# A decoder layer on one core: order of the first transfers, of a product's partner, of a gate's three steps, of spills, and of two attention lanes

## The chip, the cores and the metric

The kernel runs on one core of a Trainium2 chip. The core has five engines that work side by side, each through its own list of instructions in order: TensorE (PE, matmuls; its weight loads are shown apart as PEld), VectorE (DVE), ScalarE (ACT), GpSimd (POOL) and SyncE (SP, which here only starts transfers). SP, ACT and POOL each start transfers (DMAs) on a queue of their own. Engines wait for one another through semaphores. The metric is the device time of one execution in microseconds (us).

## What is computed

One layer of a hybrid decoder trunk, in float32, for 256 tokens of width 2048: an RMS norm, one wide projection, a gated linear attention (GLA, branch a), a differential attention (branch b), two branch projections that two gates merge, an output projection, and a residual with a second norm.

```python
h = rmsnorm(x, pre_norm_g[l])
proj = h @ w_in[l]
(a_q, a_k, a_v, a_g, a_lr, b_q, b_k, b_v, b_g, m_a, m_b) = jnp.split(proj, offsets, axis=-1)
gk = jax.nn.log_sigmoid((a_lr @ gla_gk_w2[l] + gla_gk_b[l]).astype(jnp.float32)) / GATE_LOGIT_NORMALIZER
o_a = gla_chunked(a_q, a_k, a_v, gk)                 # 4 heads of 256 keys, 512 values
o_a = rmsnorm(o_a, gla_norm_g[l]).reshape(B, S, GLA_VAL_DIM) * jax.nn.silu(a_g)
y_a = o_a @ w_branch_a[l]
...
w = p[:, :, 0] - lam * p[:, :, 1]                    # p: two causal softmaxes of a head's scores
o_b = jnp.einsum('bhqk,bkhv->bqhv', w.astype(v.dtype), v)      # 16 heads of 128 values
o_b = rmsnorm(o_b, diff_norm_g[l]) * (1.0 - lam_init)
o_b = o_b.reshape(B, S, DIFF_VAL_DIM) * jax.nn.silu(b_g)
y_b = o_b @ w_branch_b[l]
merged = jax.nn.sigmoid(m_a) * y_a + jax.nn.sigmoid(m_b) * y_b
x = x + rmsnorm(merged @ w_out[l], post_norm_g[l])
```

## The kernel before

**Splits.** Every float32 matrix is cut into a high part (`hi`) and a rest (`lo`), and a product is made of three matmuls: hi by hi, hi by lo, lo by hi. Weights arrive by DMA in tiles called `raw` (or `a`, `b`, `c` in the sets); ACT makes `hi` (L261), DVE makes `lo` (L262), then PE uses both (L437, L449). One such step, a "half", is 1024 columns or fewer. `take` keeps three halves made ahead of PE, and `load` starts the transfers two ahead, on SP. The tokens are split once in the same way into eight tiles `xs` (`prep_x`, L299).

**Phases.** First `first_joint`: sixteen steps of K, each with its piece of weights and its 256 tokens by 128 rows of x, which are loaded as the steps come (`load_x`). While the first pieces arrive, PE runs eight matmuls on ones (L343). Then two groups of GLA values, during which the small operations wait in a list of tasks, a step of each of them after a step of PE: among them `forget_gate` (log-sigmoid of both halves `hf` of the gate's input `gp`: Abs, Exp, Ln on ACT, then one DVE operation a half, L562) and `sum_operands` (sums of x tiles for the sets, whose splits `s4`, `r1`, `s2`, `r3` are L615 on ACT and L616 on DVE).

**Sets.** The middle of the run is seven "sets" (0 to 6): blocks of 1024 output columns made with seven products of half size in place of eight (numbered 1, 3, 5, 6, 2, 7, 4 in their order; `block_products`). A product has two parts t and each part two halves, so a slot is (set, product, t). The weight sums that the products want are made by the DMA itself (`accumulate`, L198: POOL starts a transfer that adds to the tile `a` or `b`) and by DVE (L206). Products 1, 3, 5, 2 have PSUM banks of their own; 6, 7 and 4 go on in the bank of product 1, so that after product 6 DVE reads the bank (`gr`, first half), and after product 7 again (`gr`, second half, L773) before product 4 may write to it. `phase_steps` lays out the order: after the two halves of a slot comes one half of the other products (queries, keys and values of both branches, computed as channel by token, `half_channel`, 16 matmuls into a bank `bg`). I call that half the slot's partner. There are fewer partners than slots; the table `skip` names the slots that go without. PE keeps the order as written there (`pinned`). An engine's list is otherwise made by a scheduler which may move an instruction past others, except those that are marked to keep the program's order, among themselves.

**Spills.** Tiles wanted much later are written to DRAM and fetched back (`spill`, `fetch`, both on POOL's queue unless said). Before the last product of the last set, the four tiles q and k of the GLA scores are fetched (L134).

**Lanes.** Later, while PE runs the projections of the GLA gates, of the last heads and of branch a, two generators `diff_lane(0)` and `diff_lane(1)` compute the differential attention, two heads (`one`, `two`) of a pair at a time, each lane its own pairs. A lane's steps for PE, with my letters: S (`scores`, L996/L997, two banks `bg`), T (`turned`, L1021, transposes of the probabilities, one bank), W (`weighted`, L1032 to L1034, one bank), and O (`turned_out`, L1051, transposes of the finished pair `ogb`, one bank, read by ACT as `obh`, L501, and then DVE as `obl`, L502). They are pushed in between runs of 24 matmuls of the projections, one step of each lane in turn (`pump`). There are four banks with the tag `bg`, given out in turn; a step that wants the fifth waits until the first one has been read.

Of the kernel before, what the change touches and what calls it, by code (L numbers as in the profile page):

```python
# [29 lines left out]
SETS = 7  # L30
# [46 lines left out]
def phase_steps():  # L77

    keys = ["v4"] + [f"{name}{hf}{c}" for hf in range(2) for name in ("k", "q") for c in range(4)]
    keys += [f"{name}{g}{c}" for g in EARLY for pair in range(2) for name in ("dq", "dk") for c in (2 * pair, 2 * pair + 1)]  # L80
    other = [(key, r, h) for key in keys for r in range(4 if key == "v4" else 1) for h in range(2)]
    slots = [(s, prod, t) for s in range(SETS) for prod in PRODUCTS for t in range(2)]
    front = [(0, prod, t) for prod in PRODUCTS[:2] for t in range(2)]
    skip = [(SETS - 1, 7, 1), (SETS - 1, 4, 1)] + [(s, prod, 0) for prod in (4, 2) for s in range(SETS - 1, 0, -1)]
    skip = skip[: len(slots) + len(front) - len(other)]
    mixed = []
    for slot in slots:
        mixed += [("set", *slot, h) for h in range(2)]
        for _ in range((slot not in skip) + (slot in front)):
            mixed.append(other.pop(0))  # L90
    return mixed + other
# [3 lines left out]
def hybrid_kernel(ctx: ExitStack, tc, xt, xn, preg, postg, w, w2, gkb, glag, lamv, diffg, ident_d, causal_d, lmask_d, out):  # L95
# [30 lines left out]
    def spill(t, name):  # L126
        count[0] += 1
        d = dram.tile(list(t.shape), t.dtype, name=f"{name}_{count[0]}")
        pool.dma_start(d, t)
        return d  # L130

    def fetch(d, name, make, queue=pool):
# [77 lines left out]
    def load(j):  # L210
        key, r, h = seq[j]
        src, size = weights(key, r)
        n = size // 2
        early = key == "v0"
        if key == "v3" and r == 0:
            for i in range(2):
                link(0, "a", i)
        count[0] += 1
        raw = raws[key, r] = wpool.tile([P, 2048], F32, tag="raw", name=f"raw_{count[0]}")
        if j == 0:  # L220
            load_x(0, 1)
        cuts = (0, n // 2, n, size) if j == 0 else (0, n, size) if j == 2 else (0, size)
        for a, b in zip(cuts, cuts[1:]):
            i = sp.dma_start(raw[:, a:b], src[:, a:b])
            if early:
                tc.keep_in_program_order(i)
        if early:
            for kt in X_LOADS[j // 2]:
                load_x(kt, 4)
# [53 lines left out]
    def load_x(kt, n, queue=sp):  # L283
        tc.keep_in_program_order(queue.dma_start(xraw[kt // 4][:, kt % 4 : kt % 4 + n, :], xt[:, kt : kt + n, :]))

    act.dma_start(preg_s, preg)
    load_x(1, 1, act)
    load_x(2, 2, act)
    act.preload_act_table_set("natural_log_exp_and_others")

    def x_ops(kt):
# [226 lines left out]
    def forget_gate():  # L518
        w2_raw = w2_tile[0]
        yield  # L520
        bank = ps("bg")
        for b in range(2):
            pe.transpose(bank[:, P * b : P * b + P], lr[:, b, :], ident)
        top = t2([P, 512], "lrh").bitcast(F32R)
        lrt = sm([P, S], "lrt", F32R, bufs=1)
        act.activation(top[:, :S], bank[:, :S], AF.Copy)
        for i in (0, 64):
            act.activation(lrt[i : i + 32, :], bank[i : i + 32, :S], AF.Copy)
            r = slice(i + 32, i + 64)
            dve.tensor_tensor(out=lrt[r, :], in0=bank[r, :S], in1=f32(top[r, :S]), op=ALU.subtract)  # L530
        w2_s = lend("s2l", "w2_s", F32R)
        top = lend("r3h", "w2h", F32R)
        r = slice(64, P)
        late = tc.keep_in_program_order
        late(act.activation(w2_s[:64, :], w2_raw[:64, :], AF.Copy))
        late(act.activation(top[r, :], w2_raw[r, :], AF.Copy))
        late(dve.tensor_tensor(out=w2_s[r, :], in0=w2_raw[r, :], in1=f32(top[r, :]), op=ALU.subtract))
        yield
        gp.extend(u([P, 2, 4, P], "gp") for _ in range(2))
        for hf in range(2):  # L540
            for c in range(2):
                bank = ps("bg")
                for i in range(2):
                    ct = 4 * hf + 2 * c + i
                    o = bank[:, S * i : S * i + S]
                    pe.matmul(o, w2_s[:, P * ct : P * ct + P], lrt, start=True, stop=True)
                for i in range(2):
                    ct = 4 * hf + 2 * c + i
                    act.activation(gp[hf][:, :, 2 * c + i, :], bank[:, S * i : S * i + S].rearrange("p (b t) -> p b t", b=2), AF.Identity, bias=gkb_s[:, ct : ct + 1])
            yield  # L550
        e = [lend(tag, "e") for tag in ("r3h", "r3l")]
        z = [t.rearrange("p b c t -> p (b c t)") for t in gp]
        for hf in range(2):
            act.activation(e[hf], z[hf], AF.Abs)
            yield
            act.activation(e[hf], e[hf], AF.Exp, scale=-1.0)
            yield
        for hf in range(2):
            act.activation(e[hf], e[hf], AF.Ln, bias=1.0)
        for hf in range(2):  # L560
            yield
            dve.scalar_tensor_tensor(out=z[hf], in0=z[hf], scalar=0.0, in1=e[hf], op0=ALU.min, op1=ALU.subtract)  # L562
        done.add("gate")
# [219 lines left out]
    pinned[0] = True  # L783
    fetched = []
    for step in phase_steps():
        if step == ("set", SETS - 1, 4, 0, 0):
            fetched = [[fetch(ts[name, hf], name, u) for name in ("q", "k")] for hf in range(2)]
        next(sets if step[0] == "set" else rest)
    for gen in (sets, rest):
# [160 lines left out]
    def place(t, d, m, h):  # L950
        tc.keep_in_program_order(sp.dma_start(f32(t[64 * h : 64 * h + 64, m]), d[64 * m : 64 * m + 64]))

    waiting = [(g, pair) for g in range(4) for pair in range(2)]

    def diff_lane(n):
# [107 lines left out]
        while ahead:  # L1063
            late = len(missing)
            while missing:
                arrive()
                yield
            if late:
                yield
            g, pair = ahead.pop()  # L1070
            one, two = (dict(g=g, h=2 * pair + i) for i in range(2))
            if last:
                turned_out(*last)
            last = g, pair
            scores(one)
            if g not in values:
                values[g] = [fetch(gspill[2 * g + 4 + i], name, u, sp) for i, name in enumerate(("dv", "ub"))]
            yield
            combine(one)
            scores(two)  # L1080
            yield
            ask()
            for work in (((turned, one), (combine, two)), ((weighted, one), (turned, two)), ((weighted, two),)):
                arrive()
                for part, w in work:
                    part(w)
                yield
# [216 lines left out]
```

## Time and profile before

| | |
|---|---|
| median of 3 runs (lowest to highest) | 1108.43 us (1108.39 to 1108.62) |
| the profiled execution, whole | 1108.06 us |
| its span in the profile | 1106.3 us |
| PE, DVE, ACT, POOL busy in the span | 99%, 78%, 61%, 12% |
| mean DMA traffic | 248 GB/s, 274.57 MB |
| granted PE clock, mean | 0.997 |

The span goes from the first to the last instruction that the profile records; 1.76 us of the profiled execution lie outside it. A row of the timeline gives start, length, engine, line, operation and tiles, the number of operations that the row joins, and in brackets how long the engine was idle before it and what it waited for. Lengths of neighbouring matmuls overlap, since they are pipelined, so PE's pace is read from start to start.

### The profile page before, as it was taken

What the parts mean: (1) busy time and instruction counts of PE and PEld (TensorE: products, weight loads), DVE (VectorE), ACT (ScalarE), POOL (GpSimd) and SP (SyncE); (2) the same over time, 40 slices, a digit from 0 to 9 for tenths busy, and PEclk for the clock granted to TensorE, in tenths of its full rate; (3) what the DMA queues carried; (4) which work ended last, traced back from release to release, by engine and by line L of the source; (5) the groups of instructions that cost most, each with busy time, mean ns of one, the idle gap of its engine ahead of it and who ended that gap; (6) DMA issues with size and microseconds to landing.
All of it is one profiled execution on the core that took longest, in us unless ns stands there. A gap on an engine that the chain in (4) does not pass through costs nothing.

```text
span 1106.3 us, 15250 instructions
## 1 busy us (share of the span) xinstructions
PE 1092.8 (99%) x5522; PEld 939.0 (85%) x5522; DVE 863.2 (78%) x1200; ACT 680.3 (61%) x989; POOL 132.1 (12%) x201
## 2 busy tenths in 40 slices
PE   9999999999999999999999999999999999999997
PEld 8999888888888888888887888889888888888886
DVE  7797987979979889798898988668877764655463
ACT  7886766666667667667675555567776653444460
POOL 0201111121021210211212100121110110000000
PEclk9999999999999999999999999999999999999999
DMA  9869979699798897997957654697898666556752
GB/s 346 297 229 326 281 260 312 157 303 300 269 312 218 307 244 248 320 241 276 298 143 276 238 186 153 204 326 262 255 277 270 215 227 211 190 190 220 270 195 76
DMA packets 58268, 274.57 MB, mean 248 GB/s; under 512 B 7824, under 2 KB 9360, under 8 KB 39248
## 3 DMA queue, kind: packets, MB, share of 16 engines
q1 hardware_dynamic: 36192, 184.18, 47.7%
q0 software_dynamic: 20992, 88.09, 28.8%
q10 hardware_dynamic: 1008, 1.32, 0.4%
q8 instruction: 43, 0.70, 0.3%
q14 instruction: 33, 0.27, 0.1%
HBM read 248.40 MB, written 25.17 MB: 247 GB/s over the span
## 4 chain that ended last, share of the span: by engine, by line
PE 97%; DVE 1%; issue 1%; DMA 0%; ACT 0%; DVEq 0%; SPq 0%; POOLq 0%; POOL 0%; ACTq 0%
PE mm L449 65%; PE bg L449 22%; PE bg L437 2%; PE mm L422 2%; PE mm L437 2%; PE bg L862 1%; PE bg L422 1%; PE bg L996 1%; PE bg L997 1%; DMA raw<-in_w_dram 0%; PE bg L1021 0%; PE bg L1034 0%; PE bg L1033 0%; PE bg L1032 0%; PE bg L1153 0%
## 5 line engine op out<-in xcount | busy, mean ns | idle before, releaser
L261 ACT ACTIVATE hi<-raw 128x1024 fp32r<-128x1024 f32 (+3 forms) x275 | 282.6, 1031 | 285.1 <-PE mm L449 175.3
L262 DVE TENSOR_TENSOR lo<-raw,hi 128x1024 fp32r<-128x1024 f32 (+3 forms) x275 | 325.9, 1187 | 147.7 <-ACT hi L261 144.4
L449 PE MATMUL mm<-hi,xs 128*128 128x512 f32 (+1 forms) x848 | 215.6, 389 | 2.2 <-DVE gr L773 1.8
L449 PEld LDWEIGHTS mm<-hi,xs 128*128 128x128 f32 x848 | 157.7, 189 | 29.0 <-issue 2.2
L449 PE MATMUL bg<-xs,hi 128*128 128x512 f32 x640 | 164.9, 390 | 0.0
L262 DVE TENSOR_TENSOR lo<-a,hi 128x1024 fp32r<-128x1024 f32 x112 | 135.2, 1221 | 10.5 <-ACT hi L261 9.3
L449 PEld LDWEIGHTS bg<-xs,hi 128*128 128x128 f32 x640 | 120.4, 188 | 23.3
L261 ACT ACTIVATE hi<-a 128x1024 fp32r<-128x1024 f32 x112 | 118.7, 1060 | 28.2 <-PE mm L449 22.0
L449 PE MATMUL mm<-lo,xs 128*128 128x512 f32 (+1 forms) x424 | 118.5, 385 | 0.1
L449 PEld LDWEIGHTS bg<-xs,lo 128*128 128x128 f32 x640 | 87.3, 191 | 6.2
L449 PEld LDWEIGHTS mm<-lo,xs 128*128 128x128 f32 x424 | 79.7, 189 | 14.9 <-DVE lo L262 0.4
L449 PE MATMUL bg<-xs,lo 128*128 128x256 f32 x640 | 89.3, 283 | 0.0
L262 DVE TENSOR_TENSOR lo<-b,hi 128x1024 fp32r<-128x1024 f32 x56 | 67.5, 1223 | 8.5 <-ACT hi L261 7.6
L261 ACT ACTIVATE hi<-b 128x1024 fp32r<-128x1024 f32 x56 | 59.3, 1061 | 18.5 <-PE mm L449 16.5
L449 PE MATMUL mm<-hi,oah 128*128 128x512 f32 x128 | 50.9, 398 | 0.0
L449 PE MATMUL mm<-hi,obh 128*128 128x512 f32 x128 | 50.4, 394 | 0.0
L449 PE MATMUL mm<-hi,oal 128*128 128x512 f32 x128 | 50.1, 391 | 0.0
L449 PE MATMUL mm<-hi,obl 128*128 128x512 f32 x128 | 49.9, 390 | 0.0
L1007 ACT ACTIVATE prob<-prob,mx,score_scale 128x128 f32<-128x128 f32 x64 | 34.2, 536 | 13.3 <-DVE mx L1002 13.1
L449 PE MATMUL mm<-hi,mh 128*128 128x512 f32 x96 | 37.5, 390 | 0.0
L449 PE MATMUL mm<-hi,ml 128*128 128x512 f32 x96 | 37.4, 390 | 0.0
L198 POOL DMA_DIRECT2D b<-in_w_dram x28 | 24.3, 868 | 108.8 <-DVE a L206 98.4
(288 smaller groups left out, 1874.5 us busy)
## 6 DMA issues: line engine op xcount, KB each, us to landing
raw<-in_w_dram SPq DMA_DIRECT2D x120, 1024.0 KB, 5.6
a<-in_w_dram POOLq DMA_DIRECT2D x28, 512.0 KB, 13.8
c<-in_w_dram SPq DMA_DIRECT2D x28, 512.0 KB, 8.8
b<-in_w_dram POOLq DMA_DIRECT2D x28, 512.0 KB, 7.9
a<-in_w_dram POOLq DMA_DIRECT2D x12, 1024.0 KB, 5.3
b<-in_w_dram POOLq DMA_DIRECT2D x12, 1024.0 KB, 7.9
raw<-in_w_dram SPq DMA_DIRECT2D x14, 832.0 KB, 7.2
dh<-dh POOLq DMA_DIRECT2D x16, 256.0 KB, 4.3
```

The lines of the kernel that those rows point to most:

```text
L198: pool.dma_start(chain[s, name, i][:, c], weights(f"set{s}", 2 + i)[0][:, c], accum_op=ALU.add)
L261: act.activation(hi_t[:, a:b], r[:, a:b], AF.Copy)
L262: dve.tensor_tensor(out=lo_t[:, a:b], in0=r[:, a:b], in1=f32(hi_t[:, a:b]), op=ALU.subtract)
L422: i = pe.matmul(out, lhs, rhs, start=first and n == 0, stop=last and n == len(pairs) - 1)
L437: i = pe.matmul(banks[g][b][:, :n], a[part][:, P * b : P * b + P], w[:, n * g : n * g + n], start=first, stop=last)
L449: i = pe.matmul(*args, **kw)
L862: pe.matmul(o, xk[:, P * c : P * c + P], xq.rearrange("p (b c t) -> p b c t", b=2, c=4)[:, :, c, :], start=i == 0, stop=i == 1)
L996: pe.matmul(banks[m][:, lo:up], q2[:, m, i2, t], kh[:, m, i2, :n], start=True, stop=False)
L997: pe.matmul(banks[m][:, lo:up], q2[:, m, i2, t], kl[:, m, i2, :n], start=False, stop=True)
L1007: act.activation(prob[m][:, lo:up], prob[m][:, lo:up], AF.Exp, scale=score_scale[:, b : b + 1], bias=mx[:, i : i + 1], accum_out=z[:, i : ...
```

## The change

Six edits: (1) `skip` drops (6, 7, 1), which so gets its partner back, and takes (6, 1, 0) instead, so that the partners between move one slot on; (2) x's first tile goes on ACT's queue ahead of the gains `preg`, and the second to fourth go on SP's between the first weight pieces; (3) spills keep the program's order among marked instructions; (4) in `forget_gate` the Ln of the second half is emitted a step later; (5) the fetch of q and k stands ahead of the last half of product 7 and not of the first half of product 4; (6) a lane doesn't begin with a pair while the other one stands between its two scores (`scoring`).

```diff
@@ -81,7 +81,7 @@
     other = [(key, r, h) for key in keys for r in range(4 if key == "v4" else 1) for h in range(2)]
     slots = [(s, prod, t) for s in range(SETS) for prod in PRODUCTS for t in range(2)]
     front = [(0, prod, t) for prod in PRODUCTS[:2] for t in range(2)]
-    skip = [(SETS - 1, 7, 1), (SETS - 1, 4, 1)] + [(s, prod, 0) for prod in (4, 2) for s in range(SETS - 1, 0, -1)]
+    skip = [(SETS - 1, 4, 1)] + [(s, prod, 0) for prod in (4, 2, 1) for s in range(SETS - 1, 0, -1)]
     skip = skip[: len(slots) + len(front) - len(other)]
     mixed = []
     for slot in slots:
@@ -126,7 +126,7 @@
     def spill(t, name):
         count[0] += 1
         d = dram.tile(list(t.shape), t.dtype, name=f"{name}_{count[0]}")
-        pool.dma_start(d, t)
+        tc.keep_in_program_order(pool.dma_start(d, t))
         return d
 
     def fetch(d, name, make, queue=pool):
@@ -217,13 +217,13 @@
                 link(0, "a", i)
         count[0] += 1
         raw = raws[key, r] = wpool.tile([P, 2048], F32, tag="raw", name=f"raw_{count[0]}")
-        if j == 0:
-            load_x(0, 1)
         cuts = (0, n // 2, n, size) if j == 0 else (0, n, size) if j == 2 else (0, size)
         for a, b in zip(cuts, cuts[1:]):
             i = sp.dma_start(raw[:, a:b], src[:, a:b])
             if early:
                 tc.keep_in_program_order(i)
+            if j == 0 and a:
+                load_x(*{n: (1, 1), size: (2, 2)}[b])
         if early:
             for kt in X_LOADS[j // 2]:
                 load_x(kt, 4)
@@ -283,9 +283,8 @@
     def load_x(kt, n, queue=sp):
         tc.keep_in_program_order(queue.dma_start(xraw[kt // 4][:, kt % 4 : kt % 4 + n, :], xt[:, kt : kt + n, :]))
 
-    act.dma_start(preg_s, preg)
-    load_x(1, 1, act)
-    load_x(2, 2, act)
+    load_x(0, 1, act)
+    tc.keep_in_program_order(act.dma_start(preg_s, preg))
     act.preload_act_table_set("natural_log_exp_and_others")
 
     def x_ops(kt):
@@ -557,7 +556,6 @@
             yield
         for hf in range(2):
             act.activation(e[hf], e[hf], AF.Ln, bias=1.0)
-        for hf in range(2):
             yield
             dve.scalar_tensor_tensor(out=z[hf], in0=z[hf], scalar=0.0, in1=e[hf], op0=ALU.min, op1=ALU.subtract)
         done.add("gate")
@@ -783,7 +781,7 @@
     pinned[0] = True
     fetched = []
     for step in phase_steps():
-        if step == ("set", SETS - 1, 4, 0, 0):
+        if step == ("set", SETS - 1, 7, 1, 1):
             fetched = [[fetch(ts[name, hf], name, u) for name in ("q", "k")] for hf in range(2)]
         next(sets if step[0] == "set" else rest)
     for gen in (sets, rest):
@@ -950,6 +948,7 @@
     def place(t, d, m, h):
         tc.keep_in_program_order(sp.dma_start(f32(t[64 * h : 64 * h + 64, m]), d[64 * m : 64 * m + 64]))
 
+    scoring = {}
     waiting = [(g, pair) for g in range(4) for pair in range(2)]
 
     def diff_lane(n):
@@ -1067,7 +1066,10 @@
                 yield
             if late:
                 yield
+            while scoring.get(1 - n):
+                yield
             g, pair = ahead.pop()
+            scoring[n] = True
             one, two = (dict(g=g, h=2 * pair + i) for i in range(2))
             if last:
                 turned_out(*last)
@@ -1079,6 +1081,7 @@
             combine(one)
             scores(two)
             yield
+            scoring[n] = False
             ask()
             for work in (((turned, one), (combine, two)), ((weighted, one), (turned, two)), ((weighted, two),)):
                 arrive()
```

**The start.** SP's list from its first transfer, before, then after (in_w is the weights, in_xt is x; x2 stands for two pieces in a row):

```order
1 L284 DMA xraw_84<-in_xt_dram 128x256
2 L224 DMA raw_134<-in_w_dram 128x416 x2
3 L224 DMA raw_134<-in_w_dram 128x832
4 L224 DMA raw_147<-in_w_dram 128x832 x2
5 L284 DMA xraw_85<-in_xt_dram 128x1024
6 L224 DMA raw_165<-in_w_dram 128x1664
7 L284 DMA xraw_86<-in_xt_dram 128x1024
```

```order
1 L222 DMA raw_133<-in_w_dram 128x416 x2
2 L284 DMA xraw_84<-in_xt_dram 128x256
3 L222 DMA raw_133<-in_w_dram 128x832
4 L284 DMA xraw_84<-in_xt_dram 128x512
5 L222 DMA raw_147<-in_w_dram 128x832 x2
6 L284 DMA xraw_85<-in_xt_dram 128x1024
```

ACT's list from its first instruction, before, then after:

```order
1 L286 DMA preg_s<-in_preg_dram 128x16
2 L284 DMA xraw_84<-in_xt_dram 128x256
3 L284 DMA xraw_84<-in_xt_dram 128x512
4 L289 ACT_TABLE_LOAD
5 L511 ACTIVATE ones_r<-ones 128x128
6 L299 ACTIVATE xs_75<-xraw_84,preg_s 128x256
7 L261 ACTIVATE hi_141<-raw_134 128x416 x2
8 L299 ACTIVATE xs_75<-xraw_84,preg_s 128x256
```

```order
1 L284 DMA xraw_84<-in_xt_dram 128x256
2 L287 DMA preg_s<-in_preg_dram 128x16
3 L288 ACT_TABLE_LOAD
4 L510 ACTIVATE ones_r<-ones 128x128
5 L261 ACTIVATE hi_141<-raw_133 128x416
6 L298 ACTIVATE xs_75<-xraw_84,preg_s 128x256
7 L261 ACTIVATE hi_141<-raw_133 128x416
8 L298 ACTIVATE xs_75<-xraw_84,preg_s 128x256
```

The second piece of weights is now the second transfer of SP, where it was the third; two x transfers of 128x256 and 128x512 went from ACT's queue to SP's, one of 128x256 the other way; and on ACT the first split of weights stands ahead of the first split of x.

**The end of product 7 in set 6.** PE's list from the last matmuls of product 7 (weights with r3) to the first ones of product 4 (weights with xs, same bank mm), before, then after:

```order
1742 L449 MATMUL mm_4814<-hi_5281,r3h 128x512
1743 L449 MATMUL mm_4814<-hi_5281,r3l 128x512
1744 L449 MATMUL mm_4814<-hi_5281,r3h 128x512
1745 L449 MATMUL mm_4814<-hi_5281,r3l 128x512
1746 L449 MATMUL mm_4814<-lo_5282,r3h 128x512 x2
1747 L449 MATMUL mm_4814<-hi_5291,xs_79 128x512 x4
1748 L449 MATMUL mm_4814<-lo_5292,xs_79 128x512 x2
1749 L449 MATMUL mm_4814<-hi_5321,xs_80 128x512 x4
1750 L449 MATMUL mm_4814<-lo_5322,xs_80 128x512 x2
```

```order
1738 L448 MATMUL mm_4813<-hi_5260,r3l 128x512
1739 L448 MATMUL mm_4813<-lo_5261,r3h 128x512 x2
1740 L448 MATMUL bg_5270<-xs_79,hi_5271 128x512 x2
1741 L448 MATMUL bg_5270<-xs_80,hi_5271 128x512 x2
1742 L448 MATMUL bg_5270<-xs_81,hi_5271 128x512 x2
1743 L448 MATMUL bg_5270<-xs_82,hi_5271 128x512
1744 L448 MATMUL bg_5270<-xs_79,lo_5272 128x256 x2
1745 L448 MATMUL bg_5270<-xs_80,lo_5272 128x256 x2
1746 L448 MATMUL bg_5270<-xs_81,lo_5272 128x256 x2
1747 L448 MATMUL bg_5270<-xs_82,lo_5272 128x256 x2
1748 L448 MATMUL bg_5270<-xs_82,hi_5271 128x512
1749 L448 MATMUL mm_4813<-hi_5291,xs_79 128x512 x4
```

Sixteen matmuls of a partner (bank bg_5270, the second half of a key tile) now stand between the two products. The DVE addition `gr` that reads the bank between them follows, in both lists, the split `lo` of product 4's first half; before, the reading `dk` of a partner's bank and one more `lo` stood ahead of it too, and they now come after it.

**A pair's change in a lane.** PE's list at one of the places where O of one lane is followed by its S S, before (the last matmul of a W, a T, then O and both scores):

```order
2401 L1034 MATMUL bg_7368<-dv_7150,prob_597_7128 128x128
2402 L1021 MATMUL bg_7383<-ident,prob_613_7216 128x128 x3
2403 L1051 MATMUL bg_7388<-ident,ogb_7243 128x128 x4
2404 L996 MATMUL bg_7399<-kh_6616,q_522_6615 128x128
2405 L997 MATMUL bg_7399<-kl_6617,q_522_6615 128x128
2406 L996 MATMUL bg_7400<-kh_6616,q_522_6615 128x128
2407 L997 MATMUL bg_7400<-kl_6617,q_522_6615 128x128
2408 L996 MATMUL bg_7399<-kh_6616,q_522_6615 128x256
2409 L997 MATMUL bg_7399<-kl_6617,q_522_6615 128x256
2410 L996 MATMUL bg_7400<-kh_6616,q_522_6615 128x256
2411 L997 MATMUL bg_7400<-kl_6617,q_522_6615 128x256
```

After, the other lane's W and T come behind the scores; the row just ahead of these is O, `L1050 MATMUL bg_7588<-ident,ogb_7431 128x128 x4`:

```order
2491 L995 MATMUL bg_7601<-kh_6375,q_489_6374 128x128
2492 L996 MATMUL bg_7601<-kl_6376,q_489_6374 128x128
2493 L995 MATMUL bg_7602<-kh_6375,q_489_6374 128x128
2494 L996 MATMUL bg_7602<-kl_6376,q_489_6374 128x128
2495 L995 MATMUL bg_7601<-kh_6375,q_489_6374 128x256
2496 L996 MATMUL bg_7601<-kl_6376,q_489_6374 128x256
2497 L995 MATMUL bg_7602<-kh_6375,q_489_6374 128x256
2498 L996 MATMUL bg_7602<-kl_6376,q_489_6374 128x256
2499 L1031 MATMUL bg_7629<-dv_7207,prob_635_7371 128x128
2500 L1032 MATMUL bg_7629<-dv_7207,prob_635_7371 128x128
2501 L1033 MATMUL bg_7629<-dv_7207,prob_635_7371 128x128
2502 L1020 MATMUL bg_7644<-ident,prob_648_7457 128x128 x3
```

Where W T O S S asked for five of the four banks in one go, with the second bank of the scores as the fifth, O S S W T does so too, with T as the fifth: T (bg_7644) takes the bank of O (bg_7588). After, the lanes go through [W T], [O S S W T], [S S W], [T O S S], [W T S S], each bracket between two runs of 24 matmuls, and the first such O, S S, W are followed by two matmuls of a projection and then T.

## The prediction

> **What bounds the kernel now.** I read the page's busy times and its chain first, then PE's waits, then the timeline at each wait.
>
> ```profile
> PE 1092.8 (99%) x5522; PEld 939.0 (85%) x5522; DVE 863.2 (78%) x1200; ACT 680.3 (61%) x989; POOL 132.1 (12%) x201
> PE 97%; DVE 1%; issue 1%; DMA 0%; ACT 0%; DVEq 0%; SPq 0%; POOLq 0%; POOL 0%; ACTq 0%
> ```
>
> PE is busy 99% of the span and is 97% of the chain that ended last. No edit takes a matmul away, so the change can only win what PE waits, and what it computes at a lower clock. The view of waits shows how little that is:
>
> ```profile
> PE mm L449 <- DVE gr L773: 1.8, 1, 1.8
> ...
> PE bg L996 <- ACT prob L1023: 1.1, 3, 0.4
> ```
>
> The columns are us in total, times, and the longest. One wait of 1.8 us for `gr`, three of some 0.36 us before the scores: two of the edits touch just these places. A wait costs more than its row says, since matmuls overlap and the clock can drop, so I read each price from start to start.
>
> **The end of product 7 in set 6 (skip).** The timeline there, and at the same place of set 5, where a partner stands between:
>
> ```profile
> 587.18 1.92 PE L449 MATMUL mm<-hi,xs 128*128 128x512 f32 x4 [1.83 <-DVE gr L773]
> ...
> 591.59 0.62 PE L449 MATMUL mm<-hi,xs 128*128 128x512 f32 x2
> ```
>
> ```profile
> 513.58 1.98 PE L449 MATMUL bg<-xs,hi 128*128 128x512 f32 x8
> ...
> 516.35 1.09 PE L449 MATMUL mm<-hi,xs 128*128 128x512 f32 x4
> ...
> 517.74 1.07 PE L449 MATMUL mm<-hi,xs 128*128 128x512 f32 x4
> ```
>
> The table of windows for the stretch behind the wait in set 6 (its last three columns are the granted PE clock, the DMA share and GB/s):
>
> ```profile
> 587.20:590.70 3.50, 3.50 (x9) 2.74 (x10) 2.32 (x4) 2.16 (x3) 2.34 (x5) 0.52 0.41 159
> ```
>
> In set 6 PE stands 1.83 us. Then the granted clock is 0.52 over the next 3.5 us: from 587.18 to 591.59 go twelve matmuls (4, 2, 4, 2) in 4.41 us, while in set 5 six take 517.74 - 516.35 = 1.39, so twelve 2.78. That is 1.63 more. The place costs 1.83 + 1.63 = 3.46 us.
>
> With the partner, sixteen matmuls of 516.35 - 513.58 = 2.77 us stand where PE stood 1.83. What DVE must do by then:
>
> ```profile
> 586.34 0.69 DVE L773 TENSOR_TENSOR gr<-mm,p 128x512 f32<-128x512 f32 x1
> ```
>
> ```profile
> 514.74 0.69 DVE L773 TENSOR_TENSOR gr<-mm,p 128x512 f32<-128x512 f32 x1
> ```
>
> In set 5 `gr` ends at 515.43, 0.92 before PE's 516.35, and there is no wait. After, set 6 has the order of set 5 with one small DVE operation fewer ahead of `gr`. So the whole 3.46 goes, and what is late next has 0.9 us to spare. Bounds: 1.83 (the half rate comes anyway) and 3.46.
>
> [...]
>
> The partner is taken from (6, 1, 0), so product 3's and 5's first halves come 2.77 us sooner. What they wait for are accumulated tiles `a`, issued by POOL; the last such issue, the slowest landing among them, and ACT's use:
>
> ```profile
> 530.34 0.86 POOL L198 DMA_DIRECT2D a<-in_w_dram  x1 [0.61 <-DVE lo L262]
> ```
>
> ```profile
> DMA to landing us min/median/max: 11.3/15.6/16.4
> ```
>
> ```profile
> 548.07 2.12 ACT L261 ACTIVATE hi<-a 128x1024 fp32r<-128x1024 f32 x2
> ```
>
> The tile landed at about 530.34 + 16.4 = 546.7; ACT takes its two halves from 548.07 and 549.1. Moved 2.77 earlier, ACT's first use would be at 545.3, and at 546.4 its second, some 0.3 short for the later-landing half. ACT works at least one half ahead of PE there, so I take nothing; if nothing covered it, 0.3. The fetches of q and k start earlier and ahead of two spills on POOL, which is 12% busy and on no chain: nothing.
>
> **The start (x and the weight pieces).** PE, then ACT:
>
> ```profile
> 5.21 1.75 PE L437 MATMUL mm<-hi,xs 128*128 128x416 f32 x4
> 7.30 1.02 PE L437 MATMUL bg<-hi,xs 128*128 128x416 f32 x4 [0.34 <-ACT hi L261]
> ...
> 8.92 0.92 PE L437 MATMUL mm<-hi,xs 128*128 128x416 f32 x4
> 9.69 0.92 PE L437 MATMUL bg<-hi,xs 128*128 128x416 f32 x4
> ```
>
> ```profile
> 4.61 0.55 ACT L261 ACTIVATE hi<-raw 128x416 fp32r<-128x416 f32 x1 [0.46 <-DMA raw<-in_w_dram]
> 6.70 0.55 ACT L261 ACTIVATE hi<-raw 128x416 fp32r<-128x416 f32 x1 [1.54 <-DMA raw<-in_w_dram]
> ```
>
> The first step's twelve matmuls run from 5.21 to 8.92. At full pace four take 9.69 - 8.92 = 0.77, 0.19 each; the first four take 1.75 against 0.92, so some 0.36 each: half rate. PE waits at 7.30 for the split of the second piece, which landed at 6.70, 2.1 after the first. After, that piece is second on its queue, with the first x tile on the other queue. If half the 2.1 us goes, it lands at 5.65 and is split by 6.2, and PE wants it at 5.21 + 4 x 0.36 = 6.65: the wait is gone. The row at 7.30 is nearly full pace, so the clock rose shortly before; I take 7.05. By then 5.1 matmuls are done, and 6.9 x 0.19 end at 8.36 instead of 8.92: **0.55**. Bounds: 0 (pieces share the DMA engines, and the next step's piece becomes late) and 1.4 (all twelve at full pace, 8.92 - 5.21 - 12 x 0.19).
>
> **The gate (one Ln moved).**
>
> ```profile
> 69.89 0.92 PE L449 MATMUL mm<-lo,xs 128*128 128x416 f32 x4
> ...
> 72.15 0.91 PE L449 MATMUL mm<-lo,xs 128*128 128x416 f32 x4
> 73.42 1.78 PE L449 MATMUL mm<-hi,xs 128*128 128x416 f32 x8 [0.36 <-ACT hi L261]
> ...
> 77.64 0.92 PE L449 MATMUL mm<-lo,xs 128*128 128x416 f32 x4
> ```
>
> ```profile
> 69.56 2.07 ACT L559 ACTIVATE e<-e 128x1024 f32<-128x1024 f32 x2
> ```
>
> ```profile
> 76.27 1.02 DVE L262 TENSOR_TENSOR lo<-raw,hi 128x832 fp32r<-128x832 f32 x1
> ```
>
> A round of lo and hi takes 72.15 - 69.89 = 2.26 undisturbed; the next two take 77.64 - 72.15 = 5.49, 0.97 too long. ACT does two Ln in a row (2.07) and is late with `hi`; with the second one behind it, `hi` comes 1 us sooner. But DVE has the same work in that stretch, and its `lo` of 76.27 ends at 77.29, only 0.35 before PE uses it at 77.64. If PE comes 0.97 sooner it waits there. So I take 0.35; bounds 0 and 0.97.
>
> **The lanes.** The scores S S at a place that waits, and at one that doesn't; the length of W; and when `obl` ends after O:
>
> ```profile
> 800.41 0.38 PE L1032 MATMUL bg<-dv,prob 128*128 128x128 f32 x2
> ...
> 801.08 0.49 PE L1021 MATMUL bg<-ident,prob 128*128 128x128 f32 x3
> ...
> 801.76 0.31 PE L996 MATMUL bg<-kh,q 128*128 128x128 f32 x1
> ...
> 803.34 1.55 PE L449 MATMUL mm<-hi,xs 128*128 128x512 f32 x6
> ```
>
> ```profile
> 815.88 0.60 PE L1051 MATMUL bg<-ident,ogb 128*128 128x128 f32 x4
> 816.24 0.31 PE L996 MATMUL bg<-kh,q 128*128 128x128 f32 x1
> ...
> 817.24 0.49 PE L1021 MATMUL bg<-ident,prob 128*128 128x128 f32 x3
> ```
>
> ```profile
> 818.01 0.75 DVE L502 SCALAR_TENSOR_TENSOR obl<-bg,diffg_s,obh 128x512 fp32r<-128x512 f32 x1
> ```
>
> ```profile
> 907.80 0.60 PE L1051 MATMUL bg<-ident,ogb 128*128 128x128 f32 x4
> ```
>
> ```profile
> 909.33 0.74 DVE L502 SCALAR_TENSOR_TENSOR obl<-bg,diffg_s,obh 128x512 fp32r<-128x512 f32 x1
> ```
>
> S S takes 803.34 - 801.76 = 1.58 where it waits and 817.24 - 816.24 = 1.00 where not: three times 0.58, **1.74** removed. But O S S W T puts a new wait in its place: T needs O's bank, and is ready 0.36 (O) + 1.00 + 0.67 (W, 801.08 - 800.41) = 2.03 after O's start. O's bank is free when `obl` ends: 2.27 after O at 907.80, 2.88 at 815.88. I take 2.27 for the two later places: there, too, DVE has only its two `lo` ahead, while at 815.88 the scores' combination pushed them back. From `gr`'s end, 587.03, to PE's 587.18 a handover takes 0.15, so T stands 2.27 + 0.15 - 2.03 = 0.39, twice. At the first place two matmuls (0.46) stand before T, and DVE has one more operation (0.69) ahead: 0.62. Together 1.40, and the net gain is **0.34**. Bounds: +1.74 (no wait) and, with 2.88 everywhere, 1.74 - 2 x 1.00 - 1.23 = -1.5. Behind PE in these waits stand its projections; nothing else is late for them.
>
> **Spills in order.** They move among POOL's instructions only. POOL is 12% busy, and what is spilled is wanted long after: nothing, bounds 0.3 either way.
>
> **Sum.** 3.46 + 0.55 + 0.35 + 0.34 = 4.7 us. The profiled execution took 1108.06, of which 1.76 lie outside the span and stay: 1103.36. The median of the runs is 0.37 above that execution, so 1103.7.
>
> **Rivals.** *The half rate isn't the gap's doing.* The clock may drop once in a while for another reason, and be elsewhere after. For it: a single gap, a single row. Against it: it starts at the gap's end, and the three runs lie within 0.23 us, though a drop that comes and goes would cost 1.63. Gain 3.1, 1105.4. [...] *T waits as after 815.88.* Lanes -1.5 in place of +0.34: 1105.6. For it: ACT or DVE may get other work in ahead of `obl`, as at that row. *The start gains nothing*, since the pieces share one set of DMA engines: 1104.3. *The edits don't do what they say*: a partner's own DVE work delays `gr`, or the gate's wait only goes from ACT to DVE. With half of set 6's gain gone and the lanes at -1.5, 1.1 is left: 1107.3, no change to be measured. *Slower: T waits very long.* One row of before shows how late `obl` can be:
>
> ```profile
> 779.38 0.60 PE L1051 MATMUL bg<-ident,ogb 128*128 128x128 f32 x4
> ```
>
> ```profile
> 784.14 0.74 DVE L502 SCALAR_TENSOR_TENSOR obl<-bg,diffg_s,obh 128x512 fp32r<-128x512 f32 x1
> ```
>
> It ends 5.50 after O, because ACT had two heads' exponentials first. At the three places T would stand 3.6 + 3.6 + 3.2 = 10.4 us, the lanes cost 8.7 net, and the whole is 1108.4 - 4.4 + 8.7 = 1112.8, more if the clock drops behind each. It turns the sign from where `obl` ends about 4.1 after O. Against it: after, the other lane's scores no longer come just before.
>
> **How the numbers follow.** Forecast (within 1 us of 1103.7) 0.45; half rate stays 0.13; T as after 815.88 0.18; nothing at the start 0.08; better than that (bounds of start, gate and lanes, up to 3 us more) 0.06; edits half undone 0.06; slower 0.04. The range takes in the rivals with 1105.4 and 1105.6, and the bounds: 1101.2 to 1106.0. A measurement tells 0.2% (2.2 us) from no change: faster 0.89, same 0.07, slower 0.04.
>
> **What the profile would show.** No wait for `gr` in set 6 and no clock under 1 there; PE's second matmul step at about 8.4, without the wait for the second piece; no wait for ACT's `hi` at 73, but a small one for DVE's `lo` a round later; no wait of scores on `prob`, and three waits of T on `obl` of 0.4 to 0.6 us. I am wrong if T's waits exceed 1 us, if a dip of the clock stays, or if a new wait for an `a` tile stands in set 6.

## The result and the profile after

The change makes the kernel faster: 1103.07 us median (1102.82 to 1103.30, 4 runs) against 1108.41 (1107.02 to 1108.62, 4 runs) on the same chip, a ratio of 0.9953, 95% interval 0.9937 to 0.9968. The profiled execution took 1102.91 us with a span of 1101.1; before it was 1108.06 and 1106.3. On another chip, in a later comparison, the ratio was 0.9956 (0.9944 to 0.9969).

The page of the changed kernel, busy times and chain, and its view of PE's waits (us in total, times, longest):

```profile
PE 1090.1 (99%) x5522; PEld 936.7 (85%) x5522; DVE 862.2 (78%) x1200; ACT 680.5 (62%) x989; POOL 132.8 (12%) x201
PE 96%; ACT 1%; DVE 1%; issue 1%; DMA 0%; DVEq 0%; POOLq 0%; POOL 0%; ACTq 0%
```

```profile
PE bg L342 <- DVE ones_b L339: 1.6, 1, 1.6
PE mm L448 <- DVE lo L262: 0.4, 1, 0.4
PE bg L1020 <- DVE obl L501: 0.3, 1, 0.3
PE mm L436 <- ACT xs L298: 0.3, 1, 0.3
```

PE still bounds everything and does the same 5522 matmuls (`L448`, `L1020` and so on are the lines called `L449`, `L1021` before). The 1.8 us for `gr` and the three waits on `prob` are gone. Three small waits stand in this view that were not there before: one for DVE's `lo`, one for `obl`, one for the first split of x. PE's busy time fell by 2.7 us with the same work, most of it from matmuls that ran at half rate before. The timeline of the changed kernel at the end of product 7 in set 6 (PE, then DVE):

```profile
581.48 1.75 PE L448 MATMUL bg<-xs,hi 128*128 128x512 f32 x7
583.07 1.12 PE L448 MATMUL bg<-xs,lo 128*128 128x256 f32 x8
...
584.25 1.09 PE L448 MATMUL mm<-hi,xs 128*128 128x512 f32 x4
```

```profile
582.10 0.68 DVE L771 TENSOR_TENSOR gr<-mm,p 128x512 f32<-128x512 f32 x1
```

The partner stands there, `gr` ends at 582.78, 1.47 before PE wants the bank at 584.25, and the four matmuls behind take 1.09, not 1.92. The start, PE and then ACT:

```profile
5.45 1.20 PE L436 MATMUL mm<-hi,xs 128*128 128x416 f32 x4 [0.26 <-ACT xs L298]
6.48 0.93 PE L436 MATMUL bg<-hi,xs 128*128 128x416 f32 x4
...
8.08 1.03 PE L436 MATMUL mm<-hi,xs 128*128 128x416 f32 x4
```

```profile
4.89 0.51 ACT L298 ACTIVATE xs<-xraw,preg_s 128x256 fp32r<-128x256 f32 x1 [0.36 <-DMA preg_s<-in_preg_dram]
```

The second step of K starts at 8.08 (8.92 before), without a wait for the second piece. The first one starts later than before (5.45, 5.21 before): its x split now waits for the gains `preg`, which come second on ACT's queue. The gate, PE, and the three T in the lanes of which two are shown, with the `obl` that each waits for:

```profile
76.66 1.02 PE L448 MATMUL mm<-lo,xs 128*128 128x416 f32 x4 [0.41 <-DVE lo L262]
```

```profile
783.56 0.55 PE L1020 MATMUL bg<-ident,prob 128*128 128x128 f32 x3 [0.32 <-DVE obl L501]
```

```profile
818.87 0.39 PE L1033 MATMUL bg<-dv,prob 128*128 128x128 f32 x2
819.38 0.55 PE L1020 MATMUL bg<-ident,prob 128*128 128x128 f32 x3
```

```profile
782.76 0.74 DVE L501 SCALAR_TENSOR_TENSOR obl<-bg,diffg_s,obh 128x512 fp32r<-128x512 f32 x1
```

```profile
818.58 0.74 DVE L501 SCALAR_TENSOR_TENSOR obl<-bg,diffg_s,obh 128x512 fp32r<-128x512 f32 x1
```

To add these up I took the time from each matmul's start to the next one's, less what that pair takes where nothing disturbs it, and summed what stands out by place (us; called the excess below). The four rows are the places that the edits touch; other places have some excess too, the same in both profiles to 0.1.

| place | before | after | gain |
|---|---|---|---|
| first 12 us | 1.68 | 0.93 | 0.75 |
| gate (66 to 80 us) | 0.97 | 0.76 | 0.21 |
| sets | 3.67 | 0.00 | 3.67 |
| lanes (770 to 912 us) | 3.79 | 3.32 | 0.47 |

Together 5.1, of a span that is 5.2 shorter. This is one execution against one; the first row and half of the third turn out below to differ from execution to execution.

### The profile page after: what moved, and what is told of

The parts are those of the page before. It is cut to its first block, busy times and chain, and to the rows that moved or that the text cites. A ratio compares the mean times of both kernels' runs of the same rounds, so it can differ in the third digit from the quotient of the medians.

```text
span 1101.1 us, 15244 instructions
## 1 busy us (share of the span) xinstructions
PE 1090.1 (99%) x5522; PEld 936.7 (85%) x5522; DVE 862.2 (78%) x1200; ACT 680.5 (62%) x989; POOL 132.8 (12%) x201
## 3 DMA queue, kind: packets, MB, share of 16 engines
q10 hardware_dynamic: 864, 1.06, 0.3%
## 4 chain that ended last, share of the span: by engine, by line
PE 96%; ACT 1%; DVE 1%; issue 1%; DMA 0%; DVEq 0%; POOLq 0%; POOL 0%; ACTq 0%
PE mm L448 64%; PE bg L448 22%; PE mm L436 2%; PE mm L421 2%; PE bg L436 2%; PE bg L860 1%; PE bg L421 1%; PE bg L996 1%; PE bg L995 1%; PE bg L1020 1%; DVE lo L262 0%; DMA preg_s<-in_preg_dram 0%; PE bg L1156 0%; PE bg L920 0%; ACT hi L261 0%
## 5 line engine op out<-in xcount | busy, mean ns | idle before, releaser
L448 PE MATMUL mm<-hi,xs 128*128 128x512 f32 (+1 forms) x848 | 214.5, 387 | 0.0
L448 PEld LDWEIGHTS mm<-hi,xs 128*128 128x128 f32 x848 | 156.7, 188 | 26.0 <-ACT hi L261 0.2
L448 PE MATMUL bg<-xs,hi 128*128 128x512 f32 x640 | 164.8, 389 | 0.0
L448 PEld LDWEIGHTS bg<-xs,hi 128*128 128x128 f32 x640 | 120.3, 188 | 23.4
L448 PE MATMUL mm<-lo,xs 128*128 128x512 f32 (+1 forms) x424 | 118.0, 383 | 0.4 <-DVE lo L262 0.4
L448 PEld LDWEIGHTS bg<-xs,lo 128*128 128x128 f32 x640 | 87.3, 190 | 6.2
L448 PEld LDWEIGHTS mm<-lo,xs 128*128 128x128 f32 x424 | 79.4, 188 | 15.3 <-DVE lo L262 0.8
L448 PE MATMUL bg<-xs,lo 128*128 128x256 f32 x640 | 89.2, 282 | 0.0
L448 PE MATMUL mm<-hi,oah 128*128 128x512 f32 x128 | 50.8, 397 | 0.0
L448 PE MATMUL mm<-hi,obh 128*128 128x512 f32 x128 | 50.4, 394 | 0.0
L448 PE MATMUL mm<-hi,oal 128*128 128x512 f32 x128 | 50.0, 390 | 0.0
L448 PE MATMUL mm<-hi,obl 128*128 128x512 f32 x128 | 49.9, 390 | 0.0
L448 PE MATMUL mm<-hi,mh 128*128 128x512 f32 x96 | 37.5, 390 | 0.0
L448 PE MATMUL mm<-hi,ml 128*128 128x512 f32 x96 | 37.4, 389 | 0.0
```

Source lines behind the costliest of these rows:

```text
L448: i = pe.matmul(*args, **kw)
```

## The experiments

**Each edit alone.** First the partner with the earlier fetch, put on the kernel before:

```diff
-    skip = [(SETS - 1, 7, 1), (SETS - 1, 4, 1)] + [(s, prod, 0) for prod in (4, 2) for s in ...]
+    skip = [(SETS - 1, 4, 1)] + [(s, prod, 0) for prod in (4, 2, 1) for s in ...]
...
-        if step == ("set", SETS - 1, 4, 0, 0):
+        if step == ("set", SETS - 1, 7, 1, 1):
```

> The kernel before with the skip table and the earlier fetch alone. Theory: the wait for gr in set 6 and the half clock behind it go, 1.99 us from start to start and 1.68 us of half rate, and nothing takes their place: 3.7 us less than before, no PE wait over 0.2 us in set 6. Rival 1: the half rate is not tied to the gap and shows up at another place: about 2.0 less. Rival 2: a tile a is late once the partner of (6, 1, 0) is gone: a new wait of some 0.3 us in set 6.

Measured: 1105.02 against 1107.82 for before (ratio 0.9978, 0.9968 to 0.9987). The wait and the half rate are gone from its profile:

```profile
583.69 1.12 PE L449 MATMUL bg<-xs,lo 128*128 128x256 f32 x8
...
584.88 1.09 PE L449 MATMUL mm<-hi,xs 128*128 128x512 f32 x4
```

The excess in the sets is 0.00 (3.67), and no wait for an `a` tile came: rivals 1 and 2 fall for this profile. The time won is 2.8, though, not 3.7; the sections on the gap's cost and on the two groups of times show why.

The start alone:

```diff
-        if j == 0:
-            load_x(0, 1)
...
+            if j == 0 and a:
+                load_x(*{n: (1, 1), size: (2, 2)}[b])
...
-    act.dma_start(preg_s, preg)
-    load_x(1, 1, act)
-    load_x(2, 2, act)
+    load_x(0, 1, act)
+    tc.keep_in_program_order(act.dma_start(preg_s, preg))
```

> The kernel before with the new order of the first transfers alone. Theory: the second step of K starts at about 8.1 us instead of 8.9 and all later steps follow it: 0.8 us less than before. In the kernel after, the first matmul waits for the first x split, which waits for the gains preg: the same wait (0.26 us at 5.4) is expected here. Rival: the start of the second step comes earlier but a later piece is late by as much: no change by 48 us (the first transposes of L522).

Measured: 1106.27 against 1107.82, ratio 0.9992 (0.9982 to 1.0002): not told from none by the time. The profile (timeline, PE):

```profile
5.58 1.57 PE L436 MATMUL mm<-hi,xs 128*128 128x416 f32 x4 [0.39 <-ACT xs L298]
6.98 0.91 PE L436 MATMUL bg<-hi,xs 128*128 128x416 f32 x4
...
8.49 0.92 PE L436 MATMUL mm<-hi,xs 128*128 128x416 f32 x4
```

The wait for the second piece is gone and the one for x and `preg` is there. The second step starts at 8.49 here, at 8.08 in the changed kernel, mostly because the clock rose later (the first four matmuls take 1.57 against 1.20). What the edit is worth thus depends on the execution. The third step of K starts between 10.84 and 11.71 in the five profiles with the old order of transfers (11.20 in that of before). In the six of this document that have this order (the start's, the changed kernel's and four of later sections) it starts between 10.46 and 10.79 five times, and at 12.55 once. Middle against middle that is some 0.5.

The gate alone:

```diff
         for hf in range(2):
             act.activation(e[hf], e[hf], AF.Ln, bias=1.0)
-        for hf in range(2):
             yield
```

> The kernel before with the two Ln apart and nothing else. Theory: PE's waits at 73.4 and 75.3 us (0.97 from start to start) are replaced by one for DVE's lo a round or two later (0.68 in the kernel after): 0.3 us less, which a time cannot tell from none; the profile must show the one wait in place of two. Rival: ACT was not the cause and the wait for hi stays: no change at all.

Measured: 1107.07 against 1107.82, ratio 0.9995 (0.9986 to 1.0005). The view of waits has one for `lo` of 0.4 us in place of the gate's wait for `hi`; the excess from 66 to 80 us is 0.77 (0.97). As expected, and too small to be seen in the time.

The lanes alone:

```diff
+            while scoring.get(1 - n):
+                yield
             g, pair = ahead.pop()
+            scoring[n] = True
...
             scores(two)
             yield
+            scoring[n] = False
```

> The kernel before with the lanes' rule alone. Theory: three waits of the scores for prob (1.57 us from start to start) are replaced by three of T for obl (0.49, 0.29 and 0.29): 0.5 us less than before. Rival: T waits as long as obl ends after O where exponentials stand ahead, over 1 us each: as slow as before or slower. In both cases the 1.8 us wait in set 6 stays.

Measured: 1106.26 against 1107.82, ratio 0.9986 (0.9977 to 0.9996). No wait on `prob`, three T that wait for `obl`; excess of the lanes 3.56 (3.79), the second T having waited 0.16 longer here than in the changed kernel. The theory holds, at 0.2 to 0.5; that the medians lie 1.6 apart is taken up with the two groups of times.

The spills in program order alone:

```diff
-        pool.dma_start(d, t)
+        tc.keep_in_program_order(pool.dma_start(d, t))
```

> The kernel before with the spills in program order alone. Theory: POOL's order changes and PE's waits stay where they were and as long: within 0.3 us of before, a half-rate stretch behind set 6's gap apart. Rival: a spill held back delays a transfer that a set waits for, a PE wait over 0.3 us that the kernel before lacks.

Measured in one run: 1107.12. PE's waits are those of before, apart from the one for the second piece of weights (0.8, 0.3 before), which comes ahead of any spill. Nothing, as expected.

**What the gap costs.** In the profiles of the last four kernels (start, gate, lanes, spills) the wait of 1.83 us in set 6 is still there, yet only the start's profile shows half rate behind it. The four matmuls behind the gap, in the start's kernel, the gate's, the lanes' and the spills':

```profile
586.80 1.83 PE L448 MATMUL mm<-hi,xs 128*128 128x512 f32 x4 [1.83 <-DVE gr L772]
```

```profile
587.41 1.15 PE L449 MATMUL mm<-hi,xs 128*128 128x512 f32 x4 [1.83 <-DVE gr L772]
```

```profile
586.82 1.15 PE L449 MATMUL mm<-hi,xs 128*128 128x512 f32 x4 [1.83 <-DVE gr L773]
```

```profile
587.72 1.16 PE L449 MATMUL mm<-hi,xs 128*128 128x512 f32 x4 [1.83 <-DVE gr L773]
```

The same gap to 0.01 us. The four matmuls behind it take 1.92 and 1.83 in two profiles (before, start), and 1.15 or 1.16 in the others. The windows view of the start's kernel and of the gate's gives the clock there (the third last column):

```profile
587.00:590.50 3.50, 3.50 (x9) 2.70 (x9) 2.40 (x3) 1.99 (x3) 2.52 (x5) 0.51 0.45 177
```

```profile
587.50:590.90 3.40, 3.40 (x16) 2.81 (x17) 2.98 (x4) 3.00 (x4) 2.32 (x5) 1.00 0.41 160
```

So I put six gaps into one program, at the end of product 7 of sets 1 to 6:

```diff
-    skip = [(SETS - 1, 4, 1)] + [(s, prod, 0) for prod in (4, 2, 1) for s in ...]
+    skip = [(SETS - 1, 4, 1)] + [(s, *p) for p in ((7, 1), (4, 0), (2, 0)) for s in ...]
```

> The kernel after with another skip table: the slots (s, 7, 1) of sets 1 to 6 go without partners, those partners stand at (s, 2, 0) as far as the count allows and at (s, 1, 0). So PE should stand some 1.8 us for gr at the end of product 7 six times, at six phases of whatever clocks the throttle. Theory 1 (every such gap costs half rate behind it): six stretches of half rate, 6 x 3.7 = 22 us more than the kernel after. [...] Theory 3 (a gap of this length never costs clock): no half rate, 6 x 2.0 = 12 us more.

Measured: 1113.42 (1113.03 to 1116.30, 4 runs) against 1106.87 (ratio 1.0067, 1.0050 to 1.0084), 10 us above the changed kernel. The first and the last of its six gaps (timeline, PE):

```profile
230.84 1.16 PE L448 MATMUL mm<-hi,xs 128*128 128x512 f32 x4 [1.29 <-DVE gr L771]
```

```profile
594.34 1.16 PE L448 MATMUL mm<-hi,xs 128*128 128x512 f32 x4 [1.83 <-DVE gr L771]
```

Five gaps came out at 1.29 us, only the last at 1.83. Behind none of the six the clock fell, and the excess in the sets is 9.71: 5 x 1.45 + 1.99, with the rest spread thin. Theory 1 falls: a gap of 1.29 us cost no clock five times over, nor did the one of 1.83. Theory 3 fits this kernel, but is contradicted by the start's kernel and by before. The last section sets the gaps of 1.83 us side by side.

**Two groups of times.** The changed kernel again, with many runs of before beside it:

> The changed kernel itself, beside many runs of before on one chip. Theory: before has a gap of 1.83 us that costs 1.7 us of half rate in some executions and nothing in others, so its times fall into two groups some 1.7 us apart; after has no such gap and only one group, apart from the clock's phase at the start. About 4 to 5 us less than before's median. Rival: the two groups have another cause (the start): after shows them too, as far apart and as often.

Measured: 1102.73 (1102.70 to 1103.21, 5 runs) against 1107.24 (9 runs), ratio 0.9956 (0.9944 to 0.9969). All 57 runs of before that were made beside these kernels fall into two groups with nothing between 1107.24 and 1107.59: 28 at 1106.09 to 1107.24, and 29 from 1107.59 up, all but four of them at 1108.64 or less. The changed kernel's nine lie at 1102.70 to 1103.30. That is what a half rate that costs 1.7 us in some executions makes, and the changed kernel has one group alone, as the theory has it. But the gap isn't the only source, so the rival is not wholly wrong: the partner's kernel, which has no gap, has seven runs at 1104.3 to 1105.6 and three at 1106.5 to 1106.6, and the kernel of the next experiment has two at 1106.4 above eight at 1104.1 to 1105.0. The profiled execution of the latter is one of the two, and shows where: PE's first step of K

```profile
5.68 1.76 PE L436 MATMUL mm<-hi,xs 128*128 128x416 f32 x4 [0.49 <-ACT xs L298]
7.23 1.59 PE L436 MATMUL bg<-hi,xs 128*128 128x416 f32 x4
8.62 0.90 PE L436 MATMUL mm<-lo,xs 128*128 128x416 f32 x2
```

runs at half rate to the end, and the second starts at 10.00 instead of 8.08. Both sources cost about the same, so times can't tell them apart: one of the upper 29 runs of before, at 1107.99, has a mean clock of 0.999, while a stretch of 3.4 us at 0.5 alone would bring the mean over 1106 us down by 0.0015, to 0.998 as it is shown here. Its length came from somewhere else. How often each of the two comes stays open.

A median of such runs depends on how many of them fall in the upper group. On the chip of the single edits, lower group against lower group (before's median there is 1106.49), the partner's kernel is 1.9 us faster, the lanes' 0.5, the start's 0.75, and the gate's not at all (0.1 slower). The groups are chosen by time here, so this is a reading, not a test. It fits 1.99 for the gap alone and the excesses of the other edits.

**What is left in the lanes.** T moved behind twelve more matmuls, wherever the other lane stands between its scores:

```diff
                 for part, w in work:
+                    if part is turned and w is two and scoring.get(1 - n):
+                        yield "go"
                     part(w)
```

> The kernel after, with T of a lane's second head moved behind twelve more matmuls wherever the other lane stands between its two scores. Theory: T waits for O's bank only because obl ends 2.3 us or more after O; 2.7 us later the bank is long free, so the three waits for obl (1.06 us together) go and no wait takes their place: 1.1 us less than the kernel after. Rival: W of the second head then waits for ACT's copy of T, which stands behind a hi split: waits of the same size at W.

Measured: 1104.71 against 1106.87; the excess of the lanes is 4.95, where the changed kernel has 3.32. The waits for `obl` are gone, and W waits three times for ACT's copy of T instead. The longest of them, with what ACT did (timeline, PE and then ACT):

```profile
813.37 0.49 PE L1031 MATMUL bg<-dv,prob 128*128 128x128 f32 x2 [1.02 <-ACT prob L1022]
```

```profile
812.26 0.58 ACT L1006 ACTIVATE prob<-prob,mx,score_scale 128x256 f32<-128x256 f32 x1
...
812.85 0.47 ACT L1022 ACTIVATE prob<-bg 128x384 f32<-128x384 f32 x1
```

The copy stands behind the other head's exponentials, not behind a split, as the rival had it. Otherwise the rival held, and for slots that had not waited before: the rule had moved T in W S S T too. With T moved only in O S S W T, where the next W has scores ahead of it (`opened` is true while a lane stands just behind its O):

```diff
                 turned_out(*last)
+                opened[n] = True
...
             yield
+            opened[n] = False
...
+                    if part is turned and n and w is two and opened.get(0):
+                        yield "go"
```

> The kernel after, with T moved behind twelve more matmuls only in the slots O S S W T, and not in W S S T as in e7_turn. Theory: no wait for obl, and since the next W stands behind other scores there, no wait for ACT's copy either: 1.06 us less than the kernel after, no PE wait over 0.1 us between 770 and 912 us. Rival: the copy is late there too, a wait of W of 0.3 us or more at each of the three places.

Measured: 1102.07 (1102.03 to 1102.27, 4 runs), ratio 0.9949 (0.9934 to 0.9964), beside 1102.73 for the changed kernel. Its profile has no PE wait between 770 and 912 us. So the bank of O was all that T waited for. The theory said 1.06 us less; the times give 0.7.

**What is left at the start and the gate.** `preg` first on ACT's queue, and one more step ahead of the split of r1:

```diff
-    load_x(0, 1, act)
     tc.keep_in_program_order(act.dma_start(preg_s, preg))
+    load_x(0, 1, act)
```

```diff
         split("s4", s4)
         yield
+        yield
         split("r1", r1)
```

> The kernel after with preg ahead of the first x tile on ACT's queue. Theory: the first matmul waits for preg alone, which landed at 4.85 us as the second transfer of that queue; ahead of x it lands earlier, x lands at most some 0.4 us later than it did, and the first matmul starts up to 0.25 us sooner, at 5.2 us, at once behind the warm matmuls. Rival: x becomes as late as preg was: no change, the first matmul at 5.4 or later.

> The kernel after, with one more step between the splits of s4 and r1. Theory: DVE has too much in the three rounds after the gate, the two gp and s4, r1, s2; one lo moves ahead of r1's split, so PE's wait of 0.41 us at 76.7 (0.68 from start to start) goes or shrinks to under 0.2. Rival: the same work only waits a round later: a wait of the same size near 78 to 81.

Measured in one run each. `preg`: 1102.63, with the first matmul at 5.34 (5.45): the split now waits for x instead,

```profile
4.78 0.51 ACT L298 ACTIVATE xs<-xraw,preg_s 128x256 fp32r<-128x256 f32 x1 [0.81 <-DMA xraw<-in_xt_dram]
```

so some 0.1 won, between the theory and its rival. The gate: 1102.37; its view of waits has none for `lo` any more, and rounds of lo and hi take 2.26 to 2.28 from 69.43 to 80.76; the theory holds, and the wait doesn't come back.

**All three together:**

> The kernel after with preg ahead of x, one more step between the splits of s4 and r1, and T moved as in e11_turn. Theory: 0.3 + 0.6 + 1.06, together 2 us less than the kernel after on the same chip. Rival: the waits come back a round later and less than 1 us remains.

Measured: 1101.43 (1100.90 to 1101.88, 5 runs), ratio to before 0.9943 (0.9931 to 0.9955), and 1.3 us under the changed kernel's 1102.73 on the same chip. That lies between the theory (2) and its rival (under 1). The waits for x, `lo` and `obl` are gone from its view of waits, apart from some 0.1 at the first matmul. A new wait of 0.2 us for a DMA (`vback`, at 722 us; 0.5 from start to start) is in the profile of this run and in no other. It takes back part of the gain, and why it came isn't settled.

## Why the prediction was right

Forecast 1103.7, measured 1103.07; the own execution 1103.36 against 1102.91. Term by term:

- **Set 6 (3.46 forecast):** by the two profiles 3.67, of which 1.99 is the gap from start to start and 1.68 the half rate. The step on what is late next was right (0.9 to spare; 1.47 measured), and so were the partner of (6, 1, 0) and the fetches at nothing. The part that was wrong is the certainty of the half rate. I argued against the first rival that a drop that comes and goes would show in three runs. The three agreed by luck: the half rate is in two of the six profiles with a gap of 1.83 us, so it does come and go. The rival was wrong in its turn to part the drop from the gap: both profiles that have it have it right behind that gap (0.14 and 0.25 us after its end), and no kernel without the gap shows any clock lost in the sets. The gain is 1.99 always and 1.68 more in some executions.
- **The start (0.55):** 0.75 in the changed kernel's profile; the wait for the second piece went as forecast. Not seen: `preg`, now behind x on its queue, became the last thing that the first matmul waits for (0.26). The clock gave it back: the four matmuls at 5.45 take 1.20 and not 1.75, since the clock rose at 5.85 in that execution and at 7.05 in before's. The prediction took 7.05 for the changed kernel too, without a reason. That the term comes out near its forecast is in part luck: over the profiles of all kernels it is some 0.5.
- **The gate (0.35):** 0.21 by excess. The step that DVE would be the limit a round later was right, with its wait of 0.41 for `lo`. With DVE's work spread by one more step, the wait went altogether.
- **The lanes (0.34):** 0.47. T waits for `obl` at the three places as forecast, and with the 2.27 that I took for `obl` the later two come out right but for the handover. That was mis-sized: from the end of `obl` (819.32) to T (819.38) it takes 0.06, not the 0.15 taken from `gr`. The three T stand 0.49, 0.29 and 0.29 too long instead of 0.62, 0.39 and 0.39. The other half of the term was too large as well: the waits of the scores that went are 1.57 from start to start, three times 0.52, not 1.74. The two errors, 0.33 and 0.17, have the same sign and so largely cancel in the difference.
- **Spills (0):** no wait of PE changed with them.

The rivals of late T (after 815.88, or the 5.5 us of 784.14) did not come: at none of the three places does T stand more than 0.5 us. The three signs of being wrong did not show either.

## What to carry to other kernels

The gap of 1.83 us on the bounding engine cost 1.99 us here in four profiles and 3.67, twice its length, in two. So look for half rate behind it in more than one profile before pricing it, and make more than three runs before arguing from their agreement. When a bank or buffer that runs short is won back by another order, look at once for the next user of the oldest one: T took the scores' place here (it stood 0.49, 0.29 and 0.29 us too long), and twelve matmuls later it did not wait. A transfer that is put ahead on a queue makes another one on it later: here it was eight kilobytes of gains, and the first matmul stood 0.26 us for the split that needs them.

## What was not expected of the hardware

**The clock behind a gap.** The same gap of 1.83 us, at the same instruction, cost 1.68 us of half rate in two profiles (before, the start's kernel) and nothing in four (gate, lanes, spills, six gaps). The traces keep the granted clock as stretches, each with a start and a length. In before the clock rises at 7.05 us and falls at 587.32, in the start's kernel it rises at 6.78 and falls at 587.05; the full rate lasts 580.27 in both, and the half rate behind it 3.413. The six gaps side by side, with the clock that the windows view gives behind each and the length of the four matmuls there (us):

| kernel | gap of PE | clock behind it | four matmuls behind it | half rate costs |
|---|---|---|---|---|
| before | 585.35 to 587.18 | 0.52 from 587.2 to 590.7 | 1.92 | 1.68 |
| start | 584.97 to 586.80 | 0.51 from 587.0 to 590.5 | 1.83 | 1.68 |
| gate | 585.58 to 587.41 | 1.00 from 587.5 to 590.9 | 1.15 | 0 |
| lanes | 584.99 to 586.82 | 1.00 from 587.0 to 590.5 | 1.15 | 0 |
| spills | 585.89 to 587.72 | 1.00 from 587.5 to 590.9 | 1.16 | 0 |
| six gaps, the last | 592.51 to 594.34 | no drop | 1.16 | 0 |

Neither the length of the gap nor the instruction behind it tells the two from the four, and when the gap comes doesn't either by itself: in the start's kernel and in the lanes' it lies within 0.02 us of the same time of the span, and only the first lost clock. What decides is not shown; there are two drops to go by, and no gap longer than 1.83 us was tried.

**The start.** In the first microseconds the granted clock reads 1.00 in the windows view (0 to 3.5 and 3.5 to 7 us of before) while matmuls run at half rate (the four at 5.21 in 1.75 us, the four at 8.92 in 0.92), so there the pace has to be read from start to start. The end of that half rate differs from execution to execution by several us (5.85 us in the changed kernel, 10.61 in the first kernel with T moved): an excess of 0.93 against 3.04 in the first 12 us, some 2 us of the whole time. What sets that end is not shown. The late one, which would be the second source of the two groups of times, rests on one execution and was not tested.
